# One transformer block on one core: attention in a hand-written order, router logits with the weights held in the array, and a first gather with the tokens held in the array

## The chip, the cores and the metric

The kernel runs on one core of one Trainium2 chip. The metric is device time in microseconds (us) of one execution; lower is better. The core has five engines that run in parallel, each through its own list of instructions in order, and wait for each other by semaphores: TensorE (PE in the rows; its weight loads, PEld, stand apart), VectorE (DVE), ScalarE (ACT), GpSimd (POOL) and SyncE (SP), which issues nearly all DMA transfers here. PE writes only to PSUM, which ACT and DVE read.

## The reference

The block works on 512 latent tokens of width 1024 with 256 context tokens. Cut to what matters:

```python
# sub-layer 1
h = modulate(rms_norm(x, g_pre1), sh1, sc1);  hc = ... the same for ctx
na_o = neighbourhood_attention(q, k, v, k_ctx, v_ctx, rpb)   # 8 heads of 64
hg_o = hgrn2_readout(...)                                    # 4 heads of 128, a scan over the tokens
mix  = jnp.concatenate([na_o, hg_o], axis=-1) @ w_out
x    = x + gt1 * rms_norm(mix, g_post1)
# sub-layer 2
h2   = modulate(rms_norm(x, g_pre2), sh2, sc2)
aff  = jax.nn.softmax(h2 @ w_router, axis=-1)                # 512 tokens x 16 experts
gate, idx = lax.top_k(aff.T, 64)                             # each expert picks its 64 best tokens
xs   = h2[idx]
y    = (silu(xs @ w_gate[e]) * (xs @ w_up[e])) @ w_down[e] * gate    # 16 experts, 1024 -> 2752 -> 1024
x    = x + gt2 * rms_norm(scatter_add(y, idx), g_post2)
```

## The kernel before

**Stages.** The first part computes the projections and the scan (until about 340 us). Then come attention and the output projection with all that follows it for the four blocks of 128 tokens (numbered j = 0 to 3), then the 16 experts one after another, whose weights (some 540 MB) stream from HBM.

**Memory.** Large tiles come from a heap of 18 slots of 1 MB (`big`). A weight tile of an expert can only be loaded when the tile that lay in its slot before has been read for the last time. Five smaller places (`wk`, `wx`) hold weight tiles too. SP issues the loads in the order in which the program names them, so a load that waits for its slot holds up those behind it. In the order of use the first expert's tiles are four for each of five steps over 512 hidden columns, two small ones for the last 192 columns, then eleven of `w_down`. In both programs 20 tiles of the first expert go in before PE has used one.

**Attention.** There are 16 units (j, hp): a block of 128 queries and a pair of heads. A unit passes through score products (`att_a`: PE, then DVE's fused add and minimum at L843 and ACT's exponential at L845), division by the sum (`att_n`, DVE L850 and L851), four transposes for each head and their copy (`att_b`, PE L856, ACT L858), and the product with the values (`att_c`, PE L867). Step n of `attention` runs these for units n, n-1, n-2 and n-3; there are 19 steps, 0 to 18. PSUM holds two score tiles and two transposed tiles at a time (`aux`, four buffers).

**Other work in those steps.** `out_state` multiplies the scan's result with its half of `w_out` (eight pieces of 12 matmuls); `finish(j)` does the attention's half (24 matmuls), the norm, the residual and the router's logits and softmax of block j; `before_last` prepares block 3; `project` does block 3's output projection head pair by head pair; `ranks_first` counts, for the first expert, how many tokens rank above each token. They are generators in the list `side`, and `tick` advances the first of them by two or three pieces a step. Up to the end of the attention the framework's scheduler may then reorder what each engine is given; from `drain()` on the program's order holds.

**Behind the attention.** `finish_last` norms block 3 and computes its logits and softmax; then `select(0)` ranks the remaining tokens, makes a one-hot matrix `hot` (tokens x 64 places) of the first expert, and `gather_one` gathers: before, 32 matmuls with a 128x128 piece of the tokens `res[j]` as the weights and 64 columns of `hot` streamed past them, the result already turned with the features on the partitions; `normed` scales it into `xT`. `expert(0)` then starts (L1291), and the second expert's gather runs in the middle of it.

In the trace a matmul of 32-bit floats leaves two records (the 32 matmuls of `gather_one` are x64); those of the split type F32R leave one.

## Time and profile before

| | us |
|---|---|
| median of 3 runs | 1773.34 (1771.5 to 1775.71) |
| the profiled execution, its own time | 1774.09 |
| its span, first to last instruction | 1772.3 |
| around the span | 1.8 |

The profiled execution is 0.75 us above the median. Times below are us from the start of its span. A row of the trace gives the start, the length, the engine and line, the operation, output <- input, shapes and a count of records that follow each other; in brackets the idle time just before and what ended it. Granted clock is that of PE as a share of 2.4 GHz.

### The profile page before, as it was taken

The page shows a single profiled execution, that of the slowest core. Times are in us where ns is not written, and L with a number is a line of the kernel's source. Part 1 is how long each engine was busy: PE and PEld are TensorE (multiplying, and loading weights), DVE is VectorE, ACT ScalarE, POOL GpSimd, SP SyncE. Part 2 cuts the span into 40 slices and gives each one's busy share as a digit, 9 for nine tenths or more (in the row PEclk, how much of TensorE's full clock was granted, in tenths as well). Part 3 has the DMA queues.
Part 4 walks back from the last instruction along what each step waited for, and adds up shares of the span by engine and source line. Part 5 has one row for each costly group of instructions (what it writes and reads, how often), then busy time and mean ns, then how long its engine had stood idle before and what let it go on. Part 6 is the DMA issues. An engine that isn't in the chain of part 4 may idle for free.

```text
span 1772.3 us, 21446 instructions
## 1 busy us (share of the span) xinstructions
PE 1598.9 (90%) x8726; PEld 840.6 (47%) x8726; DVE 599.6 (34%) x1259; ACT 343.2 (19%) x669; POOL 185.8 (10%) x291
## 2 busy tenths in 40 slices
PE   7999989999799999989898889889898988898896
PEld 5988789777643433433242334334332423343233
DVE  4787653765521311402221130204122211302023
ACT  4463331564310110101011001101100110111002
POOL 1262463622000000000000000000000000000003
PEclk9999999998799999999999999999999999999998
DMA  9463212541678999999999999999999999999995
GB/s 379 158 228 117 95 49 85 157 167 60 272 313 345 420 421 421 421 421 420 421 420 422 420 421 420 421 421 420 421 421 421 420 420 421 422 420 421 420 421 232
DMA packets 91059, 602.45 MB, mean 340 GB/s; under 512 B 12992, under 2 KB 13376, under 8 KB 23888
## 3 DMA queue, kind: packets, MB, share of 16 engines
q1 hardware_dynamic: 90176, 598.73, 82.5%
q0 software_dynamic: 784, 2.34, 0.4%
q8 instruction: 69, 1.13, 0.3%
q14 instruction: 30, 0.25, 0.0%
HBM read 598.10 MB, written 3.16 MB: 339 GB/s over the span
## 4 chain that ended last, share of the span: by engine, by line
DMA 52%; PE 29%; DVE 3%; issue 2%; POOL 2%; ACT 1%; POOLq 0%; SPq 0%; DVEq 0%; ACTq 0%
DMA w_up<-in_w_gu_dram 21%; DMA w_gate<-in_w_gu_dram 14%; DMA w_down<-in_w_dn_dram 13%; PE mm L1291 10%; PE o L1320 4%; DMA wx<-in_w_gu_dram 2%; PE aux L1188 2%; PE mm L463 2%; PE mm L802 2%; PE aux L1199 1%; PE mm L454 1%; DMA w_down<-in_w_dl_dram 1%; PE o L1356 1%; PE aux L856 1%; PE o L867 1%
## 5 line engine op out<-in xcount | busy, mean ns | idle before, releaser
L1291 PE MATMUL mm<-w_up,room 128*64 128x512 f32 (+1 forms) x1264 | 511.7, 553 | 61.4 <-DMA w_up<-in_w_gu_dram 61.4
L1291 PE MATMUL mm<-w_gate,room 128*64 128x512 f32 (+1 forms) x1152 | 453.2, 542 | 0.0
L1320 PE MATMUL o<-w_down,hidT 128*64 128x512 f32 (+1 forms) x1320 | 306.4, 600 | 25.6 <-DMA w_down<-in_w_dn_dram 24.7
L1291 PEld LDWEIGHTS mm<-w_up,room 128*64 128x64 f32 x1264 | 164.9, 138 | 227.1 <-issue 113.7
L1291 PEld LDWEIGHTS mm<-w_gate,room 128*64 128x64 f32 x1152 | 151.0, 137 | 155.4 <-issue 137.2
L1300 DVE TENSOR_TENSOR sl<-sl,mm 64x512 f32<-64x512 f32 x96 | 60.9, 634 | 441.7 <-ACT sl L1296 441.1
L1267 DVE COPY hidT<-aux 128x256 f32<-128x256 f32 x96 | 38.6, 402 | 503.4 <-PE aux L1266 503.4
L1296 ACT ACTIVATE sl<-mm 64x512 f32<-64x512 f32 x96 | 52.4, 546 | 727.4 <-PE aux L1266 574.0
L1320 PEld LDWEIGHTS o<-w_down,hidT 128*64 128x64 f32 (+1 forms) x1320 | 85.3, 136 | 222.4 <-issue 145.1
L1291 PE MATMUL mm<-wx,room 128*64 128x512 f32 x384 | 172.9, 597 | 0.0
L1291 PE MATMUL mm<-wk,room 128*64 128x512 f32 (+1 forms) x272 | 119.9, 592 | 5.8 <-DMA wk<-in_w_gu_dram 5.8
L1241 POOL COPY hot<-room 128x256 f32<-128x256 f32 x2 | 0.8, 450 | 1064.0 <-DMA wx<-in_w_gu_dram 1064.0
L454 PE MATMUL mm<-hl,whi 128*128 128x512 f32 x320 | 102.6, 399 | 0.6 <-ACT fk L709 0.6
L1328 ACT ACTIVATE y<-o 64x512 f32<-64x512 f32 x30 | 17.7, 591 | 329.8 <-PE o L1320 329.4
L1372 PE MATMUL mm<-yy,back 128*128 128x512 f32 (+1 forms) x128 | 48.0, 459 | 23.4 <-DVE sl L1300 21.7
L1291 PEld LDWEIGHTS mm<-wx,room 128*64 128x64 f32 x384 | 49.5, 136 | 39.3 <-issue 34.5
L454 PEld LDWEIGHTS mm<-hl,whi 128*128 128x128 f32 x320 | 58.8, 189 | 12.5 <-ACT fk L709 1.1
L454 PE MATMUL mm<-hl,wlo 128*128 128x512 f32 x160 | 63.0, 394 | 0.0
L1266 PEld LDWEIGHTS aux<-cc,sl 64*128 64x128 f32 x352 | 28.9, 137 | 69.4 <-issue 51.5
L1188 PE MATMUL aux<-room,res 128*128 128x128 f32 x448 | 53.7, 278 | 1.5 <-DVE room L1165 1.5
L1188 PEld LDWEIGHTS aux<-room,res 128*128 128x128 f32 x448 | 51.1, 192 | 2.5 <-issue 1.6
L1291 PEld LDWEIGHTS mm<-wk,room 128*64 128x64 f32 x272 | 33.1, 141 | 30.1 <-issue 16.6
(342 smaller groups left out, 2036.5 us busy)
## 6 DMA issues: line engine op xcount, KB each, us to landing
w_down<-in_w_dn_dram SPq DMA_DIRECT2D x150, 1024.0 KB
w_up<-in_w_gu_dram SPq DMA_DIRECT2D x128, 1024.0 KB
w_gate<-in_w_gu_dram SPq DMA_DIRECT2D x114, 1024.0 KB
wx<-in_w_gu_dram SPq DMA_DIRECT2D x48, 1024.0 KB
wk<-in_w_gu_dram SPq DMA_DIRECT2D x30, 1024.0 KB
wm<-in_w_mod_dram SPq DMA_DIRECT2D x24, 1024.0 KB
wraw<-in_w_in_dram SPq DMA_DIRECT2D x16, 1024.0 KB
w_down<-in_w_dn_dram SPq DMA_DIRECT2D x15, 768.0 KB
```

The lines of the kernel that those rows point to most:

```text
L454: T.matmul(p, w[wx][:, k, a], hT(hx, k, t0, t1), start=(n == 0), stop=(n == 3 * KT - 1))
L463: T.matmul(p, hT(hx, k, t0, t0 + 128), w[wx][:, k, :], start=(n == 0), stop=(n == 3 * KT - 1))
L802: T.matmul(p, lhs[lx][:, 2 * k2 + k], w[k2][wx][:, k, n * 512:(n + 1) * 512], start=(m == 0), stop=(m == 11))
L856: T.transpose(pT[:, i], s[:, i * 128:(i + 1) * 128], ident)
L1188: T.matmul(pX[:, k], res[j][:, (4 * k4 + k) * 128:(4 * k4 + k + 1) * 128], hot[:, 4 + j], start=(j == 0), stop=(j == 3))
L1266: T.transpose(pT[:, f], sl[:, f * 128:f * 128 + 128], ident[0:64, 0:64])
L1267: V.tensor_copy(hid[:, f0:f0 + nf], pT[:, 0:nf])
L1291: T.matmul(p[64 * g:64 * g + 64, 0:n], xe[k], ws[g][k // 4][:, k % 4, 0:n], start=(k == 0), stop=(k == KT - 1))
L1296: S.activation(sl[:, 0:n], p[0:64, 0:n], AF.Silu)
L1300: V.tensor_mul(sl[:, 0:n], sl[:, 0:n], p[64:128, 0:n])
L1320: T.matmul(pd[64 * g:64 * g + 64], hid[r, f0 + f], ww[r], start=(f0 + f == 0), stop=(f0 + f == 21))
L1372: T.matmul(p, back[:, j * 128:(j + 1) * 128], yn[i], start=(i == 0), stop=(i == 1))
```

## The change

Four things are edited.

The order of attention is written out. `att_a` falls into `att_bias`, `att_s`, `att_m` and `att_e`; in step n PE gets the scores of unit n, the value product of unit n-3 and the transposes of unit n-2, in this order; DVE divides unit n-1 and then does the minimum of unit n. The scheduler is switched off before step 2, so the program's order holds on every engine. The side work comes from a table `plan`: for each step the pieces that follow it, in order. The split of the attention's half of `w_out` into a high and a low part (`wout_split`) becomes pieces of that table, and block 3's head pairs are projected one in each of the steps 16 to 18 and one after them. The high and low parts of the heads (`nhl`) move into the heap.

The router's logits are computed with the router weights as the stationary operand: eight matmuls of 128x32 weights against 128 streamed tokens into four groups of 32 columns (`products`), a copy to SBUF, and one matmul with `sel4` that adds the four groups up and turns the result. This replaces eight matmuls with 128x128 tokens as weights and 16 streamed columns. It applies to the shift's logits, the four blocks and block 3's residual, six times in all.

The first two gathers are by token: for each j the 64 columns of `hot` are the weights and 512 columns of `res[j]` are streamed, twice (8 matmuls); ACT copies the result, PE turns it with four transposes, and `normed` scales it. For the first expert the matmuls of j = 0 to 2 are given before the last ranks.

`finish_last` gets 12 matmuls whose result nobody reads (`warm`), the ranks of the first three blocks are done in three pieces (after step 18, after the last projection, and inside `finish_last`), and one pass over the second half of block 3 moves from DVE to ACT.

```diff
+    def wout_load(k2):
         raw = big((128, 2, D), "woraw")
         nc.sync.dma_start(raw, I["w_out"][k2])
+        return raw
+
+    def wout_split(raw, to):
         hi = big((128, 2, D), "wohi", F32R)
         lo = big((128, 2, D), "wolo", F32R)
+        to.append((hi, lo))
...
+            yield
...
+    wr = np_.tile([128, KT, 32], F32, name="wr")
+    G.memset(wr, 0.0)
+    nc.sync.dma_start(wr[:, :, 0:NE], I["w_router"].rearrange("(k p) e -> p k e", p=128))
+    sel4 = np_.tile([128, NE], F32, name="sel4")
+    V.tensor_reduce(sel4, ident.rearrange("p (g c) -> p c g", g=4)[:, 0:NE], axis=mybir.AxisListType.X, op=OP.add)
...
+            if n >= 3:
+                att_c(*units[n - 3], B.pop(n - 3))
             if 0 <= n - 1 < len(units):
                 for a in A[n - 1]:
                     att_n(*a)
+            if n < len(units):
+                A[n] = att_m(p)
...
+                for a in A[n]:
+                    att_e(*a)
+            yield n
...
+    ctx.enter_context(tc.manual_schedule())
...
+    def products(x):
+
+        pl = aux((128, 128))
+        for k in range(KT):
+            g = 32 * (k % 4)
+            T.matmul(pl[g:g + 32], wr[:, k], x(k), start=(k < 4), stop=(k >= 4), tile_position=(0, g))
+        lg = np_.tile([128, 128], F32, name="lg", bufs=1)
+        V.tensor_copy(lg, pl)
+        yield
+        pr_ = aux((128, NE))
+        T.matmul(pr_, lg, sel4, start=True, stop=True)
+        yield pr_
...
+    def parts_of_heads():
+        nhl = big((128, 2, 4, 128), "nhl", F32R)
+        return nhl[:, 0], nhl[:, 1]
...
-        pr_ = aux((128, NE))
-        for k in range(KT):
-            T.matmul(pr_, hT2[:, k], wr[:, k], start=(k == 0), stop=(k == KT - 1))
-        yield pr_
+        yield
+        yield from products(lambda k: hT2[:, k])
...
+    def warm(n):
+
+        p = otl((128, 256))
+        for i in range(n):
+            T.matmul(p, ident, cc[:, 0:256], start=True, stop=True)
...
+        warm(2)
         for n, c in enumerate(halves):
             S.activation(junk, p[n], AF.Square, accum_out=q(n))
             V.tensor_mul(x1[:, c], p[n], g1[:, c])
-        products = router(x1)
-        next(products)
-        next(products)
-        c = halves[0]
-        V.scalar_tensor_tensor(junkv, x1[:, c], 2.0, xr3[:, c], op0=OP.mult, op1=OP.mult, accum_out=q(3))
-        S.activation(junk, x1[:, c], AF.Square, accum_out=q(5))
-        rnorm_of(q(0), q(1), q(2))
-        c = halves[1]
-        V.scalar_tensor_tensor(junkv, x1[:, c], 2.0, xr3[:, c], op0=OP.mult, op1=OP.mult, accum_out=q(4))
-        V.scalar_tensor_tensor(junkv, x1[:, c], 1.0, x1[:, c], op0=OP.mult, op1=OP.mult, accum_out=q(6))
-        pr_ = next(products)
+        logits = router(x1)
+        next(logits)
...
+        between()
+        next(logits)
+        pr_ = next(logits)
...
+        warm(8)
...
-        if j == 3 and hp > 1:
-            for i in range(0 if hp == 2 else hp, hp + 1):
-                project(j, i)
-        if hp == 3 and j < 3:
-            side.append(finish(j))
-            if j == 1:
-                side.append(before_last())
-            if j == 2:
-                side.extend([ranks_first(0), ranks_first(1)])
...
-    side.append(shift_logits())
-    for n, _ in enumerate(att):
-        tick(2 if n < 6 else 3)
-    ctx.enter_context(tc.manual_schedule())
-    drain()
-    finish_last()
...
+    def ranks_first():
+
+        first["row"] = row = otl()
+        first["rk"] = rk = keep.tile([128, 4, 6], F32, name="rk4")
+        G.memset(rk, 0.0)
+        spread(0, row, 0, 2)
+        ranks(0, row, rk, range(2), 0, 256, 0)
+        yield
+        spread(0, row, 2, 3)
+        ranks(0, row, rk, range(2), 256, 384, 2)
+        yield
+        ranks(0, row, rk, [2], 0, 384, 0)
+        yield
+
+    def na_weights():
+        raws = [wout_load(k2) for k2 in range(2)]
+        yield
+        for raw in raws:
+            for n, _ in enumerate(wout_split(raw, wo_na)):
+                if n % 4 == 3:
+                    yield
+
+    na_w, shift, last3, rank1 = na_weights(), shift_logits(), before_last(), ranks_first()
+    fin = [finish(j) for j in range(3)]
+    st = state_part
+    plan = {
+        2: [st, st, na_w], 3: [st, st], 4: [st, shift], 5: [st, shift], 6: [st], 7: [st, na_w],
+        8: [na_w, na_w, fin[0]], 9: [na_w, fin[0]], 10: [fin[0], fin[0]], 11: [fin[0], fin[1], last3],
+        12: [fin[0], fin[1]], 13: [fin[0], fin[1], fin[1], last3], 14: [fin[0], fin[1], last3, fin[2]],
+        15: [fin[2], fin[2], fin[1], last3], 16: [fin[2], fin[1], 0], 17: [fin[2], fin[1], 1],
+        18: [fin[2], fin[2], rank1, 2],
+    }
+    for n in att:
+        for a in plan[n]:
+            if isinstance(a, int):
+                project(3, a)
+            else:
+                next(a, None)
+    project(3, 3)
+    next(fin[2], None)
+    next(rank1)
+    finish_last(lambda: next(rank1))
...
-        def gather_one(i):
-            for k2 in range(4):
-                pX = aux((128, 2, CAP))
-                for k in range(2):
-                    for j in range(4):
-                        T.matmul(pX[:, k], res[j][:, (2 * k2 + k) * 128:(2 * k2 + k + 1) * 128], hot[:, 4 + j, i],
-                                 start=(j == 0), stop=(j == 3))
-                for k in range(2):
-                    normed(2 * k2 + k, xT[:, 2 * k2 + k, i], pX[:, k], k == 0)
+        def gather_one(i, pG, js):
+            for j in js:
+                for g in range(2):
+                    T.matmul(pG[64 * g:64 * g + 64], hot[:, 4 + j, i], res[j][:, g * 512:(g + 1) * 512],
+                             start=(j == 0), stop=(j == 3))
+            if js[-1] < 3:
+                return
+            xg = mp.tile([128, 512], F32, name="xg", tag="back", bufs=2)
+            S.activation(xg, pG, AF.Copy)
+            pX = aux((128, 4, 2, CAP))
+            for k in range(4):
+                T.transpose(pX[:, k].rearrange("p g c -> p (g c)"), xg[:, k * 128:(k + 1) * 128], ident)
+            for k in range(KT):
+                normed(k, xT[:, k, i], pX[:, k % 4, k // 4], k % 2 == 0)
...
+                pG = aux()
+                gather_one(i, pG, [0, 1, 2])
+                ranks(e, row, rk, [3], 384, 512, 4)
...
+                if i:
+                    gather_one(i, aux(), [0, 1, 2, 3])
+                else:
+                    gather_one(i, pG, [3])
```

What this does to the engines' order is seen at three places.

ACT, steps 7 to 9 of the attention. Before, the eight pieces of the second `w_out` half (`wohi`) stand in one run behind the copy `nhi` of block 0's heads (L1010), ahead of the next transposed tiles (`sT`, L858):

```order
L845 ACTIVATE s,mn<-s,mn 128x512 x2
L858 ACTIVATE sT<-aux 128x512 x2
L1010 ACTIVATE nhi<-o 128x512
L792 ACTIVATE wohi<-woraw 128x256 x8
L858 ACTIVATE sT<-aux 128x512 x2
L845 ACTIVATE s,mn<-s,mn 128x512 x2
L1023 ACTIVATE x_3249,sj<-res_3239 128x512 x2
```

Of the change, the same place:

```order
L796 ACTIVATE wohi<-woraw 128x256 x4
L880 ACTIVATE sT<-aux 128x512 x2
L869 ACTIVATE s,mn<-s,mn 128x512 x2
L796 ACTIVATE wohi<-woraw 128x256 x8
L1052 ACTIVATE nhl<-o 128x512
L880 ACTIVATE sT<-aux 128x512 x2
L869 ACTIVATE s,mn<-s,mn 128x512 x2
L796 ACTIVATE wohi<-woraw 128x256 x4
L1063 ACTIVATE x_3254,sj<-res_3244 128x512
```

The last four pieces now stand behind the exponentials of unit 9 (L869), and block 0's first squares (L1063), which need the product with them, right behind.

DVE, from the high and low parts of block 3's last heads to the first pass over block 3. Before (`nlo` are the low parts, L1107 and L1110 the ranks, L1067 the first pass, over `mm`, block 3's projection):

```order
L1002 TENSOR_SCALAR affs<-affs,sm 128x16
L1107 TENSOR_SCALAR cmp,rk_4327<-o,affs 128x384
L1110 SCALAR_TENSOR_TENSOR cmp,rk_4327<-o,affs,bef 128x384
L973 TENSOR_TENSOR nlo<-o,nhi 128x128
L1107 TENSOR_SCALAR cmp,rk_4327<-o,affs 128x384
L1110 SCALAR_TENSOR_TENSOR cmp,rk_4327<-o,affs,bef 128x384
L1067 TENSOR_TENSOR res_3240<-mm,gx 128x512
```

Of the change:

```order
L1157 SCALAR_TENSOR_TENSOR cmp,rk_4338<-o,affs,bef 128x256
L1019 TENSOR_TENSOR nhl<-o,nhl 128x128 x2
L190 TENSOR_SCALAR rsx<-sj 128x1
L1077 SCALAR_TENSOR_TENSOR affs<-aux,rsx,cr 128x16
L1040 TENSOR_REDUCE sm<-affs 128x1
L1044 RECIPROCAL sm<-sm 128x1
L1045 TENSOR_SCALAR affs<-affs,sm 128x16
L1154 TENSOR_SCALAR cmp,rk_4338<-o,affs 128x128
L1157 SCALAR_TENSOR_TENSOR cmp,rk_4338<-o,affs,bef 128x128
L1154 TENSOR_SCALAR cmp,rk_4338<-o,affs 128x128
L1157 SCALAR_TENSOR_TENSOR cmp,rk_4338<-o,affs,bef 128x128
L1113 TENSOR_TENSOR res_3245<-mm,gx 128x512 x2
```

Block 2's softmax (L1077 to L1045) and four rank instructions now stand between the last low parts and the first pass; before, the softmax stood ahead of the last low part.

PE, from block 3's last projection to the first expert. Before (L987 transposes block 3, L992 its logits, L1116 spreads its affinities, L1199 the gather):

```order
L979 MATMUL mm<-wohi,nlo 128x512
L987 MATMUL aux<-cc,res_3240 128x128 x8
L992 MATMUL aux<-wr,hT_4360 128x16 x8
L1116 MATMUL o<-cc,affs 128x128
L1199 MATMUL aux<-room,res_3239 128x64 x2
L1199 MATMUL aux<-room,res_3240 128x64 x2
```

Of the change:

```order
L994 MATMUL aux<-sel_2994,lg 128x16
L1163 MATMUL o<-cc,affs 128x128
L1101 MATMUL o<-cc 128x256 x2
L1033 MATMUL aux<-cc,res_3245 128x128 x8
L1101 MATMUL o<-cc 128x256 x2
L989 MATMUL aux<-hT_4386,wr 32x128 x8
L994 MATMUL aux<-sel_2994,lg 128x16
L1101 MATMUL o<-cc 128x256 x8
L1163 MATMUL o<-cc,affs 128x128
L1258 MATMUL aux<-res_3244,room 64x512 x4
L1258 MATMUL aux<-res_3245,room 64x512 x4
L1266 MATMUL aux<-cc,xg 128x128 x4
```

The gather is 8 matmuls and 4 transposes in place of 32 matmuls, and the unread ones (L1101) stand around the logits.

## Rows read from the trace of the kernel before

**Rows 1.** The page, the span in 40 equal slices: what the DMA engines moved.

```profile
GB/s 379 158 228 117 95 49 85 157 167 60 272 313 345 420 421 421 421 421 420 421 420 422 420 421 420 421 421 420 421 421 421 420 420 421 422 420 421 420 421 232
```

**Rows 2.** Busy time of each engine in stretches: stretch and its length, busy us (count) of PE, PEld, DVE, ACT and POOL, granted clock, DMA share, GB/s.

```profile
470.00:475.00 5.00, 0.47 (x1) 0.18 (x1) 3.85 (x17) 1.74 (x6) 0.77 (x1) 0.50 0.91 362
480.00:485.00 5.00, 5.00 (x25) 5.00 (x25) 0.61 (x2) 0.81 (x2) 0.00 (x0) 0.50 1.02 431
490.00:495.00 5.00, 5.00 (x16) 2.14 (x17) 0.34 (x1) 1.69 (x2) 0.00 (x0) 0.50 0.00 0
...
535.00:540.00 5.00, 5.00 (x38) 2.75 (x36) 1.28 (x3) 0.97 (x2) 0.00 (x0) 1.00 0.78 267
```

**Rows 3.** SP's issues of weight loads: start, length.

```profile
473.29 0.38 SPq L1286 DMA_DIRECT2D w_up<-in_w_gu_dram  x1
497.14 3.76 SPq L1277 DMA_DIRECT2D wk<-in_w_gu_dram  x2
...
534.26 0.33 SPq L1286 DMA_DIRECT2D w_up<-in_w_gu_dram  x1
```

**Rows 4.** The chain of work that ended last, from the first gather to the first matmul with `w_down`: start, length, what.

```profile
476.89 1.54 PE aux L1199 x6
478.44 12.64 PE aux L1199 x58
491.08 9.47 PE mm L1291 x32
...
501.13 7.02 PE mm L1291 x32
...
523.35 7.29 PE aux L1199 x64
...
542.66 5.30 PE o L1320 x24
```

**Rows 5.** The same chain in attention, the start of step 3 (first row), step 4 (the next five) and the start of step 8 (last).

```profile
348.31 0.63 PE aux L836 x4
...
357.08 0.63 PE aux L836 x4
357.71 0.43 PE aux L838 x4
358.15 1.02 PE aux L856 x8
359.17 1.02 PE o L867 x16
360.19 5.66 PE mm L802 x24
...
388.45 0.63 PE aux L836 x4
```

**Rows 6.** Groups of instructions by line and shape from 329 to 480 us: busy us, mean ns of one | idle time before.

```profile
L845 ACT ACTIVATE s<-s,mn 128x512 f32<-128x512 f32 x32 | 22.8, 715 | 17.5 <-DVE mn L843 17.5
L843 DVE CUSTOM_DVE_ANT_0 s<-aux,bias 128x512 f32<-128x512 f32 x32 | 21.0, 687 | 18.6 <-PE aux L838 18.4
L851 DVE TENSOR_SCALAR s<-s,mn 128x512 f32<-128x512 f32 x32 | 19.6, 623 | 0.8
L858 ACT ACTIVATE sT<-aux 128x512 f32<-128x512 f32 x32 | 17.7, 582 | 4.0 <-PE aux L856 4.0
L793 DVE TENSOR_TENSOR wolo<-woraw,wohi 128x256 fp32r<-128x256 f32 x32 | 15.8, 561 | 1.9 <-ACT wohi L792 1.9
L1110 DVE SCALAR_TENSOR_TENSOR cmp<-o,affs,bef 128x384 bf16<-128x384 f32 x4 | 2.5, 616 | 0.1
L1110 DVE SCALAR_TENSOR_TENSOR cmp<-o,affs,bef 128x128 bf16<-128x128 f32 x4 | 1.4, 344 | 0.0
```

**Rows 7.** Timeline of PE: 16 records (8 matmuls) of router logits; 24 records (12 matmuls) with weights of 32 columns in four column groups and 256 streamed columns, early in the kernel.

```profile
435.48 1.96 PE L992 MATMUL aux<-wr,hT 128*128 128x16 f32 x16
38.63 1.50 PE L274 MATMUL o<-wm,sc 128*32 128x256 f32 x24
```

**Rows 8.** PE's granted clock in two stretches of attention (columns as in rows 2), and eight transposes at either clock (timeline).

```profile
400.00:410.00 10.00, 9.91 (x47) 7.34 (x46) 5.18 (x17) 4.77 (x12) 2.59 (x4) 0.66 0.00 0
...
420.00:430.00 10.00, 8.96 (x49) 6.97 (x49) 4.90 (x18) 6.11 (x18) 3.37 (x6) 0.72 0.15 52
...
380.62 1.09 PE L856 MATMUL aux<-cc,s 128*128 128x128 f32 x8
397.32 1.02 PE L867 MATMUL o<-sT,vo 128*64 128x128 f32 x7 [0.92 <-ACT sT L858]
403.50 1.97 PE L856 MATMUL aux<-cc,s 128*128 128x128 f32 x8
```

**Rows 9.** Timeline from the end of block 3's projection to the first one-hot matrix: the first instruction of block 2's softmax, the last projection, the first pass, block 3's affinities, the one-hot of blocks 0 to 2.

```profile
456.51 0.23 DVE L1038 SCALAR_TENSOR_TENSOR affs<-aux,rsx,cr 128x16 f32<-128x16 f32 x1 [1.85 <-PE aux L992]
463.58 0.39 PE L979 MATMUL mm<-wohi,nlo 128*128 128x512 f32 x1
464.09 0.69 DVE L1067 TENSOR_TENSOR res<-mm,gx 128x512 f32<-128x512 f32 x1 [0.31 <-ACT x L1066]
472.01 0.23 DVE L1002 TENSOR_SCALAR affs<-affs,sm 128x16 f32<-128x16 f32 x1
476.48 0.36 DVE L1165 TENSOR_TENSOR room<-room,rsx 128x192 f32<-128x192 f32 x1
```

More of the change, by code (lines that the diff above doesn't have):

```diff
@@ L793, in wout @@
             V.tensor_sub(lo[:, k, c], raw[:, k, c], hi[:, k, c].bitcast(F32))
-        return hi, lo
+            yield
+    def wout(k2):
+        to = []
+        for _ in wout_split(wout_load(k2), to):
+            pass
+        return to[0]
     def outproj(p, lhs, w, n):
@@ L827, in att_a @@
         win = cc[:, C_WIN + 32 * var:C_WIN + 32 * var + 32]
-        pa = [slice(64 * g, 64 * g + 64) for g in range(2)]
         for g in range(2):
@@ L832, in att_a, with att_s @@
                          rpb[:, 2 * hp + g, off:off + 256].rearrange("p (r b c) -> p r b c", r=8, b=4))
+    def att_s(j, hp):
+        c0 = (0, 8, 24, 32)[j]
+        pa = [slice(64 * g, 64 * g + 64) for g in range(2)]
         p = [aux(), aux()]
@@ L868, in att_c @@
                          start=(i == 0), stop=(i == 3))
+    units = [(j, hp) for j in range(4) for hp in range(4)]
     def attention():
-        units = [(j, hp) for j in range(4) for hp in range(4)]
         A, B = {}, {}
@@ L965, in moe_block @@
     early = {}
+    def parts_of_heads():
+        nhl = big((128, 2, 4, 128), "nhl", F32R)
+        return nhl[:, 0], nhl[:, 1]
     def project(j, hp):
         if hp == 0:
-            early[j] = ([np_.tile([128, 4, 128], F32R, name=nm, bufs=1) for nm in ("nhi", "nlo")], [mmt(), mmt()])
+            early[j] = (parts_of_heads(), [mmt(), mmt()])
         (nhi, nlo), p = early[j]
@@ L1012, in finish @@
         nc.gpsimd.dma_start(xr1, I["xb"][j * 128:(j + 1) * 128, :])
-        if not wo_na:
-            wo_na.extend([wout(0), wout(1)])
         yield
@@ L1118, in moe_block @@
     first = {}
[L1120 to L1147 removed]
+    def ranks_first():
[4 more added lines that the diff above has]
+        ranks(0, row, rk, range(2), 0, 256, 0)
+        yield
+        spread(0, row, 2, 3)
[9 more added lines that the diff above has]
+                if n % 4 == 3:
+                    yield
+    na_w, shift, last3, rank1 = na_weights(), shift_logits(), before_last(), ranks_first()
[18 more added lines that the diff above has]
+    finish_last(lambda: next(rank1))
     if "aff" in dbg:
@@ L1209, in select @@
                 ranks(e, row, rk, [3], 0, 384, 0)
-                ranks(e, row, rk, range(3), 384, 512, 2)
+                ranks(e, row, rk, range(3), 384, 512, 4)
                 one_hot(hot, rk, i, 0, 3)
-                ranks(e, row, rk, [3], 384, 512, 2)
+                pG = aux()
+                gather_one(i, pG, [0, 1, 2])
+                ranks(e, row, rk, [3], 384, 512, 4)
                 last_factor()
```

56 lines of the change are left out of this document (22 added, 34 removed).

## The prediction, made before the changed kernel ran

> **What bounds the kernel now.** First the DMA row of the page: from the fourteenth slice on, some 575 us, the transfers run at 420 to 422 GB/s and hardly vary [rows 1]. That part moves expert weights and the change does not touch it, so the end is fixed by the moment from which the stream has no more gaps. Next the stretches around that moment: the stream stands still at 490 to 495 us and moves 267 GB/s at 535 to 540 [rows 2]. Who makes the gaps is seen in SP's issues: after the 20 tiles of the first expert (the last issued at 473.29) the next goes out at 497.14, when the first matmuls have read their tiles, and one at 534.26, after the second gather [rows 3]. So PE frees the slots late. The chain that ended last says the same: from the first gather at 476.89 to the first `w_down` matmul at 542.66 it is PE's [rows 4]. Whatever brings PE earlier to that matmul brings the end earlier by as much, as long as the 20 tiles are there in time. I therefore sum what the change does to PE up to there, in three parts, against the profiled execution; its 1774.09 us lie 0.75 above the median and 1.8 above its span, and I apply the sum to the median.
>
> **Part 1, attention up to the end of block 3's projection (t0).** Before, t0 is 463.58 + 0.39 = 463.97 [rows 9].
> One unit costs PE 0.63 + 0.43 + 1.02 + 1.02 = 3.10 us, a piece of 12 matmuls of the output projection half of 5.66, 2.83 [rows 5]. DVE has 2 x (0.69 + 0.62) a unit [rows 6], with small ones some 3.15; ACT 2 x (0.72 + 0.58) = 2.6.
> New logits: a row of weights 32 columns wide has 1.50 us for 12 matmuls over 256 streamed columns, so eight over 256 cost 1.0 and, if time goes with columns, 0.5 over 128; the old eight cost 1.96 [rows 7]. I take 0.5 plus 0.25 for the sum with `sel4`; the saving is 1.2 each (0.7 at the upper bound). The copy between them is a DVE instruction with other PE work behind it.
> Steps 3 to 7 are PE's: 3.10 + 5.66 = 8.8 for step 3 (before 357.08 - 348.31 = 8.8 [rows 5]), then 6.4 and 6.2 (one piece and the shift's logits), 5.9 and 5.9. From 348.3, step 8 starts at 381.5. The old step 8 starts at 388.45 [rows 5], but two projection pieces (5.7) are done by then that the new one still has; the rest, 1.2, is the saved logits.
> From step 8 I add each step's PE work and the waits that its order makes:
> Steps 8 and 9, 14.4. PE has only 3.1 + 6.1, but the second projection piece needs the last four split pieces, and these stand on ACT behind unit 9's exponentials. DVE: 3.15, eight pieces at 0.56 [rows 6] (some of it hidden in ACT's) and a 0.69 low part come to 7.9; the next unit brings 11.0; exponentials, four pieces and DVE's half of them end at 13.2, five matmuls at 14.4.
> Step 10, 6.1 (PE). Step 11, 5.9: the next scores need the buffers that DVE's minimum frees, and DVE has an addition and two multiplications (2.3 to 2.5) ahead of its 3.15. Step 12, 7.1 (3.10 + transposes 1.03 + 2.97) and step 13, 7.6 (PE). Step 14, 5.0 (DVE, as step 11). Step 15, 11.5: two projection pieces wait 1.2 for block 2's low part on DVE, then 5.9, transposes and a sum. Steps 16 and 17, 5.8 and 5.0: each projection of a head pair waits for its low part behind finishing work on DVE. Step 18 and the last head pair, 8.4: transposes, their copies, logits, then DVE's four ranks over 256 columns (about 1.9, between the 0.34 and 0.62 of [rows 6]) ahead of the last two low parts, then ten matmuls.
> Sum 76.8, t0 = 458.3, 5.7 earlier.
> The clock: before, PE was granted 0.66 of full speed at 400 to 410 and 0.72 at 420 to 430; eight transposes took 1.97 us instead of 1.09 there, after a wait of 0.92 for ACT [rows 8]. These 6.2 us are in the old time, and in mine none is. The new order has longer waits but no logits of 16 columns; I charge 0.7, a quarter of one such dip: **part 1 is -5.0**. Bounds: -10 (steps 8, 9 and 15 at their PE work) and 0 (the old stalls and dips come back, or half a microsecond more in each of eleven steps).
>
> **Part 2, from t0 to the end of the first cut.** Before: 463.97 to 472.24 for block 3's affinities, to 476.84 for the first one-hot matrix [rows 9], 491.08 for the first expert matmul and 500.55 for the end of its first cut [rows 4]: 8.3, 12.9, 27.1 and 36.6 after t0.
> The change puts block 2's sum and softmax (before from 456.51 on [rows 9], ahead of t0), the spread and four ranks of 128 columns ahead of the first pass on DVE: 2.0 + 0.4 + 4 x 0.29, so the pass starts 3.6 after t0 instead of 0.1. Inside the chain, two ranks of 384 columns (1.25) and a copy come in, and the shorter logits and a pass that moved to ACT go out; I count +0.2. The one-hot matrix is there at 12.9 + 3.5 + 0.2 = 16.6 after t0.
> The gather: 64 records took 14.19 us, at 0.50 of the clock all through, and the same 64 take 7.29 at full clock [rows 2, 4]. Sixteen records of 512 columns cost 7.02 / 32 x 16 = 3.5 at full clock, twice that at half; then ACT's copy 0.6, four transposes 0.5, the first `normed` 0.4, half a microsecond of handing over: 5.5, or 9 at half throughout. PE stands idle for some 4 us ahead of it, as before, when the clock was at 0.50 from 470 on [rows 2]; the unread matmuls end well before. But the old first cut took 9.47 us against 7.02 of the next [rows 4], so the clock came back within it; the new gather is work of that cut's kind and should begin to bring it back itself. I take 6.4.
> The Trainium skill, TensorE: Matmul & The Clock Gate, section Why this matters for your kernels, says the same of the idle time (it drops the clock) and would begin the gather at half rate in spite of the unread matmuls; by it this term is up to 7.5, by the unread matmuls alone 5.5. The row at 470 us speaks for the page.
> So the first expert matmul starts 23.0 after t0 (-4.1), and its cut takes 7.1 instead of 9.47 (-2.4): **part 2 is -6.5**. Bounds: -7.5 (full clock) and -1.2 (half clock through gather and cut).
>
> **Part 3, to the first `w_down` matmul.** The second gather falls from 7.29 to 3.5 + copy, transposes and scaling with their waits, 5.0, which PE takes in order: **-2.3**. Its six other cuts are unchanged.
>
> **Are the tiles there?** Slots come free in another order, 12 tiles instead of 11 at the end of attention. By the order of SP's loads the first of them waits for the projection in step 17, about 450, and the rest for t0 and what follows it, the last for ACT's final squares at t0 + 13. At 1 MB in 2.5 us (421 GB/s) 12 take 30, so they are in at 481, while the first cut ends near 489 and the tiles of the last full cut are wanted 20 us later. Eight microseconds of slack: hidden.
> Around all this, `memset`, `sel4` and the second reads cost nothing: POOL and DVE are idle there. The unread matmuls cost PE time in which it waits.
>
> **Sum.** -5.0 - 6.5 - 2.3 = -13.8: 1773.34 - 13.8 = 1759.5 us. On the profiled execution: span 1758.5.
>
> **Rivals.**
> More waits than I count: the program's order leaves no engine a way around a late operand, and every step has one or two hand-overs that I take as 0.1 to 0.2. At t0 no earlier than before, 464 to 468, parts 2 and 3 remain: 1764 to 1769. For it: the old order was made to dodge such waits and still had 0.5 to 1 us stalls [rows 8].
> Fewer: if steps 8, 9 and 15 hide their waits and the clock stays up, t0 is 453 to 455 and the gain 19 to 25, until the weight stream itself binds: 1749 to 1754. For it: DVE and ACT are half idle on the average.
> Slower, by the clock in steps 8 to 18: PE has some 63 us of full-clock work there, and at half clock each costs another. To turn -13.8 into +3.6 it takes 17 us of it at half, three times the 6.2 lost before [rows 8]. For it: the waits in steps 8, 9, 11 and 14 leave PE half idle for 4 us at a time. Time: 1778 or more. The skill's page on the clock gate speaks for this case, since it makes idle stretches the cause; in the rows dips of 10 us followed on stalls of about 1.
> No change, because the gap at 535 to 540 is not PE's but that of the slots' order, and the stream starts no earlier: 1773. Against it: the load at 534.26 goes out just when the cut after the gather has read its tile [rows 3, 4].
>
> **How the numbers follow.** The sum as worked out, 1754 to 1764: 0.50, which gives the predicted time. More waits, 1764 to 1769.8: 0.22. Fewer, below 1754: 0.18. Within 0.2% (3.5 us, about what a measurement of this kernel can tell from no change): 0.06. Slower: 0.04. Faster is then 0.90. The range 1750 to 1769 leaves out the two last, some 0.04 of each neighbour, and nothing of the first.
>
> **What would show it.** Right: block 3's last projection ends at 455 to 462; step 9's projection waits for split pieces; the one-hot matrix follows 16 to 17 us after t0; the first expert matmul 22 to 25 after it; the first cut near 7 us; the second gather 5. Wrong: a granted clock near 0.5 for more than 10 us in steps 8 to 18, a stream that stands still in front of the first cut for want of slots, or a time that changes in the experts' part.

## The result, and the profile after

| | before | changed |
|---|---|---|
| median | 1774.15 us | 1763.4 us |
| range of the runs | 1771.5 to 1776.02 | 1762.4 to 1767.99 |
| ratio, 95% interval | | 0.9946 (0.9931 to 0.9961) |
| span of the profiled execution | 1772.3 us | 1761.5 us |

The change makes the kernel 10.7 us faster by the medians, 10.8 by the spans and 9.6 by the ratio, which compares the means. Forecast were 13.8 us and 1759.5.

The bound is still the weight stream. Here are stretches of the changed kernel (columns as in [rows 2]):

```profile
475.00:480.00 5.00, 1.56 (x6) 0.59 (x8) 4.43 (x25) 0.00 (x0) 0.55 (x1) 0.93 1.00 416
480.00:485.00 5.00, 4.24 (x16) 1.29 (x12) 0.00 (x0) 0.60 (x1) 0.00 (x0) 0.73 0.98 413
490.00:495.00 5.00, 5.00 (x26) 1.76 (x24) 1.46 (x4) 0.59 (x1) 0.00 (x0) 1.00 0.67 203
535.00:540.00 5.00, 5.00 (x26) 1.69 (x24) 0.29 (x1) 0.00 (x0) 0.00 (x0) 1.00 0.53 187
```

At 480 us the granted clock, 0.50 before, is 0.73, and at 490 the stream is running again. The issues of SP that answer to [rows 3] (start, length):

```profile
474.52 0.33 SPq L1357 DMA_DIRECT2D w_up<-in_w_gu_dram  x1
489.37 3.76 SPq L1348 DMA_DIRECT2D wk<-in_w_gu_dram  x2
...
524.14 0.33 SPq L1357 DMA_DIRECT2D w_up<-in_w_gu_dram  x1
```

After the first expert's last tile the next load goes out at 489.37 in place of 497.14. The chain that ended last, as in [rows 4]:

```profile
478.44 5.37 PE aux L1258 x16
483.89 0.61 ACT xg L1263
484.54 0.67 PE aux L1266 x4
485.24 0.41 ACT room L1240
485.69 7.09 PE mm L1362 x32
...
515.58 3.61 PE aux L1258 x16
519.21 0.61 ACT xg L1263
519.86 0.66 PE aux L1266 x4
520.52 7.02 PE mm L1362 x32
...
532.54 5.30 PE o L1391 x24
```

The first gather (L1258) starts 1.55 us later than before, but its matmuls, the copy, the transposes and the scaling take 7.25 us in place of 14.2, the first cut (L1362) 7.09 in place of 9.47 and the second gather 4.94 in place of 7.29. The first `w_down` matmul is at 532.54, 10.1 us earlier, and the end with it.

Attention, in which the prediction put 5.0 us, gives less. The last projection of block 3 ends at 461.7 (before 463.97 [rows 9]):

```profile
450.12 0.50 PE L1025 MATMUL mm<-wohi,nhl 128*128 128x512 f32 x1 [2.42 <-ACT nhl L1018]
...
457.86 0.73 PE L1025 MATMUL mm<-wohi,nhl 128*128 128x512 f32 x2 [2.00 <-DVE nhl L1019]
...
461.09 0.63 PE L1025 MATMUL mm<-wohi,nhl 128*128 128x512 f32 x1
```

These are PE's waits in steps 17 and 18 and the last matmul of the projection. DVE's first pass over block 3 (L1113) starts 3.2 us after t0, and the first one-hot matrix (L1226) is ready 16.7 after it:

```profile
464.91 1.28 DVE L1113 TENSOR_TENSOR res<-mm,gx 128x512 f32<-128x512 f32 x2
...
478.02 0.36 DVE L1226 TENSOR_TENSOR room<-room,rsx 128x192 f32<-128x192 f32 x1
```

### The profile page after: what moved, and what is told of

It reads as the page before. It is cut to its first block, busy times and chain, and to the rows that moved or that the text cites. A ratio compares the mean times of both kernels' runs of the same rounds, so it can differ in the third digit from the quotient of the medians.

```text
span 1761.5 us, 21371 instructions
## 1 busy us (share of the span) xinstructions
PE 1574.5 (89%) x8674; PEld 813.5 (46%) x8674; DVE 597.6 (34%) x1272; ACT 345.4 (20%) x673; POOL 185.4 (11%) x293
## 4 chain that ended last, share of the span: by engine, by line
DMA 47%; PE 33%; DVE 4%; issue 2%; POOL 2%; ACT 2%; POOLq 0%; SPq 0%; DVEq 0%; ACTq 0%
DMA w_gate<-in_w_gu_dram 18%; DMA w_up<-in_w_gu_dram 17%; PE mm L1362 13%; DMA w_down<-in_w_dn_dram 11%; PE o L1391 4%; PE aux L1249 3%; PE mm L812 2%; PE mm L463 2%; DMA wx<-in_w_gu_dram 1%; PE mm L454 1%; PE o L1427 1%; PE aux L1337 1%; DVE wolo L797 1%; PE o L889 1%; DMA woraw<-in_w_out_dram 1%
## 5 line engine op out<-in xcount | busy, mean ns | idle before, releaser
L1362 PE MATMUL mm<-w_up,room 128*64 128x512 f32 (+1 forms) x1264 | 506.9, 548 | 64.1 <-DMA w_up<-in_w_gu_dram 64.1
L1362 PE MATMUL mm<-w_gate,room 128*64 128x512 f32 (+1 forms) x1152 | 453.8, 542 | 0.0
L1362 PEld LDWEIGHTS mm<-w_up,room 128*64 128x64 f32 x1264 | 163.6, 137 | 224.6 <-DMA w_up<-in_w_gu_dram 115.1
L1362 PEld LDWEIGHTS mm<-w_gate,room 128*64 128x64 f32 x1152 | 151.1, 137 | 159.0 <-issue 141.2
L1362 PE MATMUL mm<-wx,room 128*64 128x512 f32 x384 | 172.9, 597 | 0.0
L1362 PE MATMUL mm<-wk,room 128*64 128x512 f32 (+1 forms) x272 | 114.4, 568 | 6.3 <-DMA wk<-in_w_gu_dram 5.8
L1362 PEld LDWEIGHTS mm<-wx,room 128*64 128x64 f32 x384 | 49.5, 136 | 39.8 <-issue 35.0
L454 PEld LDWEIGHTS mm<-hl,whi 128*128 128x128 f32 x320 | 58.8, 189 | 12.9 <-ACT fk L709 1.6
L463 PE MATMUL mm<-whi,hl 128*128 128x256 f32 x256 | 47.2, 286 | 0.0
```

The lines of the kernel that those rows point to most:

```text
L454: T.matmul(p, w[wx][:, k, a], hT(hx, k, t0, t1), start=(n == 0), stop=(n == 3 * KT - 1))
L463: T.matmul(p, hT(hx, k, t0, t0 + 128), w[wx][:, k, :], start=(n == 0), stop=(n == 3 * KT - 1))
L1362: T.matmul(p[64 * g:64 * g + 64, 0:n], xe[k], ws[g][k // 4][:, k % 4, 0:n], start=(k == 0), stop=(k == KT - 1))
```

## The experiments

The start of step 3 of attention lies between 348.2 and 351.7 us in the profiles of all kernels, though the code ahead of it is the same or nearly so; the last section has part of the reason. The stretches below therefore count from there, read from PE's timeline: from the first score matmul of step 3 to t0, to the first gather matmul, to the first expert matmul, to the first `w_down` matmul, and their sum. The end came 1229 to 1231 us after that last point in all 14 profiles, so the sum stands for the part of the time that the edits reach. Where a median is given, the kernel before measured 1774.2 to 1775.4 beside it.

| kernel | to t0 | to gather | to expert | to `w_down` | sum | ratio to before (95%) |
|---|---|---|---|---|---|---|
| before | 115.7 | 12.9 | 14.1 | 51.6 | 194.4 | 1 |
| changed | 112.7 | 16.7 | 7.3 | 46.8 | 183.5 | 0.9946 (0.9931 to 0.9961) |
| e1_old_logits | 120.6 | 13.6 | 7.1 | 46.8 | 188.1 | 0.9976 (0.9967 to 0.9985) |
| e2_old_gather | 115.7 | 16.6 | 14.1 | 50.9 | 197.3 | 1.0015 (1.0005 to 1.0025) |
| e3_no_warm | 112.5 | 16.5 | 8.0 | 46.8 | 183.8 | 0.9949 (0.9935 to 0.9964) |
| e4_order_only | 120.5 | 13.9 | 14.1 | 50.2 | 198.8 | 1.0039 (1.0027 to 1.0052) |
| e5_before_gather | 115.7 | 12.9 | 8.3 | 46.8 | 183.7 | 0.9942 (0.9930 to 0.9955) |
| e6_before_logits | 109.5 | 14.8 | 14.0 | 50.3 | 188.6 | 0.9985 (0.9976 to 0.9994) |
| e7_split_early | 114.1 | 15.3 | 7.3 | 46.8 | 183.5 | 0.9942 (0.9930 to 0.9955) |
| e8_ranks_moved | 109.7 | 15.5 | 8.0 | 46.8 | 180.1 | 0.9939 (0.9926 to 0.9953) |
| e9_more_warm | 112.6 | 16.8 | 5.6 | 46.8 | 181.7 | 0.9935 (0.9923 to 0.9948) |
| e10_together | 111.2 | 17.2 | 5.6 | 46.8 | 180.7 | 0.9927 (0.9906 to 0.9947) |
| e11_before_logits_gather | 109.5 | 14.8 | 8.2 | 46.8 | 179.2 | 0.9919 (0.9907 to 0.9932) |
| e12_before_all_warm | 109.5 | 14.5 | 5.6 | 46.8 | 176.3 | 0.9901 (0.9885 to 0.9917) |

The question was which of the four edits the gain belongs to: my sum gave 5.0 to attention and the logits, 8.8 to what stands behind them.

**One edit taken back.**

e1_old_logits:

```diff
-        pl = aux((128, 128))
...
+        pr_ = aux((128, NE))
+        for k in range(KT):
+            T.matmul(pr_, x(k), wr[:, k, 0:NE], start=(k == 0), stop=(k == KT - 1))
+        yield
         yield pr_
```

> The changed kernel with the router's logits taken back to eight matmuls of 16 streamed columns with the tokens as weights, and no copy and second matmul; nothing else. Theory A (the sum of parts): each of the six costs PE 1.2 us more, of which those in steps where PE waits anyway are hidden, so 4 to 7 us more than the change: 1767 to 1770, and the granted clock stays near 1.00 in attention. Rival B (the narrow matmuls are what takes the clock away): stretches of 5 us and more at 0.50 come back around the logits of blocks 0 and 1, as at 400 and 424 us before, and the time is 1772 or more.

Measured 0.9976: 5.3 us more than the change (0.0030 of 1774), which is Theory A's. One stretch of low clock came back (0.56 to 0.59 from 398 to 402), not two. e4_order_only (0.50 from 400 to 402) and, with the new logits, e2_old_gather (0.50 too) lost it at the same place, so in the written order the narrow matmuls are not needed for that.

e2_old_gather: the loop of 32 matmuls from the kernel before in `gather_one`, called once for each expert.

> The changed kernel with both first gathers taken back to 32 matmuls with the tokens as weights and 64 streamed columns; the unread matmuls stay. Theory A: the gather runs at half the clock again, 14.2 us in place of 7.25, the first cut 9.5 in place of 7.1, the second gather 7.3 in place of 4.9; about 11 more, 1773 to 1775, all of the measured gain of the change. Rival B (the unread matmuls keep the clock): the first gather takes 7.3 to 9, the time is 1766 to 1768.

Measured 1.0015: the gain is gone and a little more. The gather takes 14.1 us, at a granted clock of 0.50 from 484 to 498, in spite of the unread matmuls. Rival B falls. Theory A's 11 us are in the profile, 6.9 in the gather and 4.1 behind it; 3.0 more are in the stretch to t0, whose instructions are those of the changed kernel.

e3_no_warm: the calls of `warm` taken out.

> The changed kernel without the 12 matmuls that nobody reads. Theory A: the clock is at half for the 4 us in front of the gather with or without them; the gather may lose the 1.8 us that it now has over half clock and the first cut up to 2.4: 0 to +4, 1763 to 1767. Rival B (they keep PE at full clock for block 3's transposes, logits and the gather): more than +4, and block 3's transposes and logits get longer too.

Measured 0.9949, no difference that can be told from the change. The gather takes 8.0 us in place of 7.3, the cut 7.09 as with them: Theory A, at its low end, though not for its reason. Without the unread matmuls the granted clock is 0.50 from 462 to 485 us, through most of the gather; with them it is 1.00 from 470 up to the gather and falls within it, as shown under part 2 below. Block 3's logits (L989) take 1.41 us in place of 0.64, its transposes 1.94 in both, and the stretch to the gather is no longer for it (16.5).

e4_order_only: the edits of e1, e2 and e3 at once.

> The changed kernel with old logits, old gathers and no unread matmuls: what stays of the change is the written order, the moved ranks and the pass on ACT. Theory A: from the two traces the order ends block 3's projection 2.3 us earlier, but that holds the logits' 4 to 6; and the moved softmax and ranks put the one-hot matrix 3.8 us later after it. So it is slower than the kernel before: 1777 to 1783. Rival B (the order is worth something by itself, since no clock dips remain in it): 1768 to 1774.

Measured 1.0039, 7 us slower than before. So the order, the moved ranks and the pass on ACT together lose time: Theory A.

**One edit alone on the kernel before.**

e5_before_gather: the new `gather_one` and its calls, put into the kernel before.

> The kernel before with the new gathers alone. Theory A: the first gather at half clock takes 9 in place of 14.2 us, the first cut 7 to 9.5, the second gather 4.9 in place of 7.3: 7.5 to 10 us off, 1764 to 1767, so nearly all that the whole change gives. Rival B (the gain needs the order and the unread matmuls): 2.4 to 5 us off, 1769 to 1772.

Measured 0.9942, 10.3 us off and as much as the whole change: Theory A, just past its range. The chain, first and second gather with the cut behind each, and the first `w_down` matmul:

```profile
477.85 6.41 PE aux L1197 x16
484.35 0.60 ACT xg L1202
485.00 0.67 PE aux L1205 x4
486.15 7.09 PE mm L1301 x32
...
516.04 3.61 PE aux L1197 x16
...
533.00 5.30 PE o L1330 x24
```

Even from half the clock (6.41 us for 16 records that take 3.61 later), the gather ends 5.8 us sooner than the old one, and the cut behind it runs at full clock.

e6_before_logits: `products`, `wr` with 32 columns and `sel4`, put into the kernel before; `nhi` and `nlo` move into the heap, since the pool has no room for the new tiles otherwise.

> The kernel before with the new logits alone (the heads' high and low parts lie in the heap as in the change, since the room is not there otherwise). Theory A: 1.2 us for each of the logits that PE does not hide, 4 to 6 off, 1768 to 1770. Rival B (the narrow matmuls take the clock away): the stretches at 0.50 around 400 and 424 us vanish too, 8 to 11 off, 1763 to 1766. Rival C (the copy between the two products is a wait that takes back what they save): within 2 of the time before.

Measured 0.9985, 2.7 us off, less than Theory A's 4 to 6. In the profile t0 is 6.2 sooner and no clock is lost where it was lost before, which is Rival B's sign without its price (columns as in [rows 8]):

```profile
400.00:410.00 10.00, 9.31 (x73) 6.66 (x74) 5.88 (x18) 4.70 (x12) 3.08 (x5) 1.00 0.61 238
420.00:430.00 10.00, 8.28 (x70) 5.57 (x71) 6.45 (x21) 7.43 (x20) 3.05 (x5) 1.00 0.11 44
```

The same stretches in e5_before_gather, which has the old logits:

```profile
400.00:410.00 10.00, 10.00 (x50) 7.58 (x50) 4.19 (x14) 3.77 (x10) 1.59 (x3) 0.66 0.00 0
420.00:430.00 10.00, 8.18 (x47) 6.22 (x46) 5.01 (x16) 6.39 (x19) 3.11 (x5) 0.77 0.16 54
```

In the scheduler's order the lost clock goes with the old logits: the two profiles that have them (before and e5) needed 115.7 us to t0, the three with the new ones (e6, e11 and e12) lost no clock up to t0 and needed 109.5. PE's rows of logits in that stretch take 5.9 us in place of 11.4. How much of the 6.2 is this, how much the clock, and how much the other order that the scheduler makes of the new rows, can't be told.

But the stretch to the gather grows by 1.8: there the second product of block 3's logits stands on the path and waits for the copy between the two:

```profile
465.82 0.40 PE L967 MATMUL aux<-sel,lg 128*128 128x16 f32 x2 [2.48 <-DVE lg L965]
```

The median gains less than the sum's 5.8: step 3 begins 1.9 us later in this profile than in that of the kernel before, which the sum leaves out, and the profiled execution lies 1.5 us below the median of its eleven.

e11_before_logits_gather: both of them.

> The kernel before with the new logits and the new gathers together, so the change without its written order, without the moved ranks and without unread matmuls. Measured from step 3 to the first matmul with w_down, the gathers alone gave 10.7 us and the logits alone 5.8, the whole change 10.9. Theory A (they add up, and the written order takes the logits' part back): 16 off, 1757 to 1759, faster than the change. Rival B (the two share a gain, that of the clock in front of the first expert, or the tiles are not there sooner): 1762 to 1764, as the change.

Measured 0.9919, some 1760, 4.8 us better than the change: Theory A, just past its range (15.1 of its 16 us by the sum). What the change has besides, the written order with the moved ranks, the unread matmuls and the pass on ACT, costs these 4.8. Two other pairs say the same: the changed kernel with old logits lies 6.0 above e5 (0.9976 and 0.9942), and e4, which has the order, the ranks and the pass alone, 6.9 above the kernel before. By the sums of the table the three pairs give 4.2, 4.4 and 4.4. No run has the written order without the other two; e8_ranks_moved, below, bears on that. PE's waits, from step 3 to t0, show where. First the changed kernel (what waited, for what: us in total, times, longest):

```profile
PE mm L812 <- ACT wohi L796: 2.8, 1, 2.8
PE mm L1025 <- ACT nhl L1018: 2.4, 1, 2.4
PE mm L1025 <- DVE nhl L1019: 2.0, 1, 2.0
PE mm L812 <- ACT nhl L1052: 1.8, 2, 1.3
```

Then the kernel with the old order and the new logits:

```profile
PE o L870 <- ACT sT L861: 1.7, 3, 0.9
PE aux L839 <- ACT sT L861: 0.8, 1, 0.8
PE mm L802 <- ACT nhl L1023: 0.7, 1, 0.7
```

And PE's busy time in the same stretch (columns as in [rows 2]), changed kernel first:

```profile
349.01:461.72 112.71, 99.27 (x777) 74.83 (x776) 60.67 (x180) 61.94 (x157) 23.91 (x37) 0.99 0.31 118
```

```profile
349.30:458.77 109.47, 104.27 (x778) 75.38 (x777) 63.21 (x179) 61.77 (x158) 23.66 (x34) 1.00 0.30 109
```

The written order makes PE idle for 13.4 us (112.71 - 99.27) where the scheduler's has 5.2. It gets 5.0 of that back in busy time, with the same matmuls in longer runs of one kind: the products with the values take 20.3 us in 16 runs in the written order, 26.3 in 24 runs in the scheduler's. That the longer runs are the reason is not shown.

**The waits of the written order.**

e7_split_early:

```diff
-        2: [st, st, na_w], 3: [st, st], 4: [st, shift], 5: [st, shift], 6: [st], 7: [st, na_w],
-        8: [na_w, na_w, fin[0]], 9: [na_w, fin[0]],
+        2: [st, st, na_w], 3: [st, st], 4: [st, shift], 5: [st, shift, na_w], 6: [st, na_w], 7: [st, na_w],
+        8: [na_w, fin[0]], 9: [fin[0]],
```

> The changed kernel with the four pieces of wout_split one or two steps earlier in the plan (steps 5, 6, 7 and 8 in place of 7, 8, 8 and 9). Theory A: PE waits 1.3 and 2.8 us in step 9 for the heads' high part and for the split pieces behind the exponentials on ACT; without that block 3's projection ends 4 us earlier, and so does all that follows: 1758.5 to 1760. Rival B: the pieces take DVE and ACT in steps 5 to 8 as much as they did in 8 and 9, or steps 11 and 14 wait the longer: 1762 to 1764.

Measured 0.9942, the sum unchanged: Rival B by the time, for a reason that neither named. PE's wait moves to step 7 (2.36 us, for the minimum on DVE), where DVE stands in front of the first low part of the second weight:

```profile
376.84 1.43 DVE L797 TENSOR_TENSOR wolo<-woraw,wohi 128x256 fp32r<-128x256 f32 x4 [6.64 <-PE aux L854]
```

That `wolo` lies in the heap slot of `qb0`, the queries of blocks 0 and 1, whose last reader is the score product of step 7 (L854); no plan of these pieces alone can have it sooner. (In this profile the clock was lost at 380 and 452 us too, so what the earlier pieces would have gained without that stays open.)

e8_ranks_moved:

```diff
-        18: [fin[2], fin[2], rank1, 2],
+        18: [fin[2], fin[2], rank1],
...
-    project(3, 3)
-    next(fin[2], None)
-    next(rank1)
-    finish_last(lambda: next(rank1))
+    project(3, 2, 0)
+    project(3, 3, 0)
+    next(fin[2], None)
+    project(3, 2, 1)
+    project(3, 3, 1)
+    next(rank1)
+    finish_last(lambda: (next(rank1), next(rank1)))
```

Here `rank1` yields once more after its first spread, and `project` with 0 does the high and low part, with 1 the matmuls.

> The changed kernel with another order around the last two head pairs: both low parts of block 3 first, block 2's sum and softmax next, then the projections of the two head pairs, the four ranks over 256 columns beside them, and the four over 128 columns after the first passes. Theory A: the projection no longer waits 2.0 us for the low part behind ranks, and the first pass no longer 3.3 us for block 2's softmax and ranks: 4 to 5 us off, 1758 to 1760. Rival B: the ranks only change their place on DVE, whose chain to the one-hot matrix is the bound: the time from step 3 to the one-hot matrix falls by less than 2, 1761.5 to 1764.

In the profile t0 is 3.0 sooner and the stretch to the gather 1.2 shorter, 4.2 in all, as Theory A has it; the gather lost 0.7 of it to the clock. The ratio is 0.9939 beside 0.9946, a gain of 1.2 us within the intervals, which is Rival B's time: the profile has the gain in one execution, the times do not show it. With 109.7 us to t0 the written order is here level with the scheduler's (109.5 in e6 and e11). So in this profile what the change loses ahead of t0 hangs on the place of the ranks and the clock behind their wait, not on the order of the attention; by the ratios (0.9939 and 0.9919) 3.5 us still lie between this kernel and e11.

e9_more_warm:

```diff
                 spread(e, row, 3, 4)
+                warm(9)
```

> The changed kernel with nine more unread matmuls behind the last spread of affinities, so that PE is busy up to the first gather. Theory A (the clock falls because PE waits 4.1 us for the one-hot matrix): the gather's matmuls take 3.6 in place of 5.4 us, 1761 to 1762.5. Rival B: unread matmuls don't hold the clock, or they end late and the gather starts later: 1763 to 1765.

```profile
481.06 3.68 PE aux L1258 x16
```

The gather's matmuls take 3.68 us in place of 5.37, and the steps up to the first expert 5.6 in place of 7.3: Theory A. The ratio, 0.9935, is 2 us lower, within the intervals.

e10_together: e8 and e9 at once.

> The changed kernel with the new place of the ranks and the nine further unread matmuls at once. From step 3 to the first w_down matmul the one measured 3.4 less than the change, the other 1.8. Theory A (they add up): 178.3 us from step 3, and 1759 to 1761 measured beside 1774 to 1775 before. Rival B: the ranks' new place leaves PE idle elsewhere, the clock falls there, and the unread matmuls run at half and delay the gather: 180 to 182 from step 3, 1762 to 1764.

Measured 0.9927, 1761.27, at the edge of Theory A's range, but the sum is Rival B's 180.7. PE at the sum of block 3's logits, and the unread matmuls behind it:

```profile
467.93 0.61 PE L994 MATMUL aux<-sel,lg 128*128 128x16 f32 x2 [2.22 <-DVE lg L991]
468.38 5.10 PE L1104 MATMUL o<-cc 128*128 128x256 f32 x16
473.31 0.27 PE L1166 MATMUL o<-cc,affs 128*128 128x128 f32 x1
```

The ranks now keep DVE from the logits' copy and PE waits 2.22 us. Behind that its clock is at 0.50, the eight unread matmuls take 5.10 us instead of the 3.70 of the changed kernel, and the spread of the affinities (L1166) stands behind them. That is Rival B's path, but the wait alone does not make it: e8_ranks_moved has the same instructions up to there and the same wait, and the clock stayed at 1.00:

```profile
468.04 0.40 PE L994 MATMUL aux<-sel,lg 128*128 128x16 f32 x2 [2.22 <-DVE lg L991]
468.28 3.70 PE L1104 MATMUL o<-cc 128*128 128x256 f32 x16
```

The stretch to t0 is 1.5 us longer than in e8, with the clock at 0.57 from 396 to 400, where e8 had 1.00. So whether the two edits add up is not settled by this profile.

e12_before_all_warm: e11 with unread matmuls in the four waits behind block 3's projection.

```diff
         V.tensor_copy(lg, pl)
+        if fill[0]:
+            warm(fill[0])
...
+        warm(2)
         logits = router(x1)
+        fill[0] = 4
...
+                warm(5)
                 spread(e, row, 3, 4)
+                warm(8)
```

> The kernel before with new logits, new gathers and unread matmuls in the four waits of PE between block 3's projection and the first gather (2, 4, 5 and 8 of them), in the old order of the attention and of the ranks. Logits and gathers alone measured 179.2 us from step 3, with the gather at half the clock from its start (8.2 us for its three steps). Theory A: at full clock these take 5.5, the other things stay: 176.5 from step 3, 1756.5 to 1758.5. Rival B: the first unread matmuls run at half the clock themselves and hold up the spread and the gather: 178 to 181, 1759 to 1762.

Measured 0.9901, 1758.06 (1756.09 to 1758.59): better than the kernel before and the changed one, and the sum, 176.3, is that of Theory A. In the profile no stretch of attention or of the work behind it lost the clock. The gather of e11, then that of this kernel:

```profile
473.53 6.33 PE L1210 MATMUL aux<-res,room 128*64 128x512 f32 x16 [4.21 <-DVE room L1178]
```

```profile
473.33 3.65 PE L1222 MATMUL aux<-res,room 128*64 128x512 f32 x16 [0.66 <-DVE room L1190]
```

It takes 3.65 us behind work and 6.33 behind a wait of 4.21.

## Why the prediction was right, and where it was not

**What bounds the kernel** held: the end kept its distance of 1230 us from the first `w_down` matmul in every profile, and the tiles were there in time. The last of the first expert's 20 was issued at 474.52 and the stream ran until 485, four microseconds later than I had it, with no cut waiting.

**Part 1** is the term that was mis-sized: -5.0 forecast, -2.3 by the absolute t0, -3.0 from step 3. Its steps held up to the end of step 16: step 8 starts 32.8 us after step 3 (forecast 33.2), step 10 47.7 (47.6, with the waits of 1.3 and 2.8 us in step 9 that the sum has), step 15 79.0 (79.3), step 17 96.4 (96.6). The miss is in the last two. "Steps 16 and 17, 5.8 and 5.0": step 17 took 6.3, since PE waits 2.42 not for the low part on DVE but for the high part on ACT (L1018), which stands behind squares and the softmax's exponential. "Step 18 and the last head pair, 8.4": 10.0; the four ranks made a wait of 2.00 as forecast, but the ten matmuls behind it took 3.9 us, against some 2.5 at full clock in e8 (12 in 3.0). Of the clock I charged 0.7 for all steps; in this profile it cost nothing in steps 3 to 16 and about 1.4 here. That is in part luck: of the four profiles with these instructions three (the change, e3 and e9) took 112.5 to 112.7 us to t0, the fourth (e2) 115.7, as long as the kernel before.

What the sum hid is that part 1 holds two things of opposite sign. I priced the logits' saving and the order's waits in one row of steps and never asked what the order does without the logits. The rival with more waits named the reason, "the program's order leaves no engine a way around a late operand", but I gave it to a t0 no earlier than before. The runs show it, together with the moved ranks and the pass on ACT, as a loss of 4 to 7 us in each pair, covered by the logits; how much of it is the order's own stays open (e8).

**Part 2** (-6.5, measured -5.5: 31.1 from t0 to the end of the first cut in place of 36.6) was right in two of its steps: one-hot matrix 16.7 after t0 (16.6), cut 7.09 (7.1). The third, the gather, took 7.25 against 6.4, and not on the path that I gave it, from half the clock upwards. PE had waited 4.1 us for the one-hot matrix; the gather then began at full clock, fell to half about a microsecond later, with PE busy, and was back at full by 483 us (columns as in [rows 2]):

```profile
478.50:479.00 0.50, 0.50 (x4) 0.22 (x6) 0.50 (x6) 0.00 (x0) 0.00 (x0) 1.00 1.01 426
480.00:481.00 1.00, 1.00 (x4) 0.24 (x2) 0.00 (x0) 0.00 (x0) 0.00 (x0) 0.50 1.09 459
483.00:484.00 1.00, 0.79 (x4) 0.00 (x0) 0.00 (x0) 0.11 (x1) 0.00 (x0) 1.00 1.01 426
```

In e9 and e12, in which PE has work up to the gather, its steps took 5.6 us, the 5.5 of the other case. The page of the Trainium skill (TensorE: Matmul & The Clock Gate, Why this matters for your kernels), which has idle time take the clock, gave up to 7.5 for the change and was nearer than my value, though the gather did not begin at half rate.

One bound of part 2 was worked out wrongly: half the clock through gather and cut would be 9 and 14.0 us, some 3 us more than before and not 1.2 less. No profile came near it.

**Part 3** was exact: 4.94 for the second gather, -2.35.

**The rivals.** "Slower, by the clock in steps 8 to 18" did not come in the profile of the change, but its mechanism exists: e2_old_gather has the same instructions up to the gather and needed 3.0 us more to t0, with the clock lost three times. That the change does nothing falls with e5. The case of fewer waits was added up wrongly: a t0 of 453 to 455 with the other parts as forecast gains 18 to 20 us, not 19 to 25. The measured time lies within the likeliest case, 1754 to 1764, at its upper end. The six signs set down for it all came, the first at its edge (461.7 of 455 to 462).

## What to carry to other kernels

Ask of every edit in a bundle what it does alone, and with its companions already there: here a written order that, with its moved ranks, lost 4 to 7 us hid behind two edits that gained. Taking those edits back one at a time showed each gain; the loss showed only where the order stood alone (e4) or its companions stood without it (e11). When a short product stands alone between two waits, turn it so that few matmuls stream many columns, and fill the wait ahead of it on PE with work whose result nobody reads, if that work ends before the operand comes. Before moving a piece earlier in an order, look up who last read the buffer it writes to.

## What the runs showed of the hardware that was not expected

The same instructions keep or lose PE's clock from one execution to the next. From 395 to 405 us the changed kernel and e2_old_gather, which is 2.0 us behind there, run the same order (columns as in [rows 2]); first the changed kernel:

```profile
395.00:405.00 10.00, 9.66 (x76) 7.19 (x77) 6.50 (x18) 4.84 (x13) 0.00 (x0) 1.00 0.12 29
```

```profile
395.00:405.00 10.00, 7.65 (x45) 5.73 (x46) 5.28 (x17) 5.31 (x15) 1.41 (x2) 0.83 0.01 2
```

The granted clock is 1.00 in the one and 0.83 in the other, part of it at 0.50. The same goes for the part ahead of attention; the changed kernel and e3_no_warm, whose code is the same there:

```profile
245.00:250.00 5.00, 4.41 (x33) 4.20 (x33) 2.35 (x8) 0.38 (x1) 5.00 (x14) 1.00 0.01 3
```

```profile
245.00:250.00 5.00, 3.38 (x12) 3.38 (x13) 1.72 (x6) 0.00 (x0) 5.00 (x15) 0.66 0.01 3
```

Step 3 starts at 349.0 and 351.5 in these two, so 2.5 of the 3.3 us between their spans arose before the edited code began. The clock is not all of it: e6_before_logits lost none from 40 to 345 us and began step 3 at 350.1. A profile's absolute times should not be compared without a common start. Nor did every wait in PE's work cost the clock: after one of 2.83 us that ended at 395 it stayed at 1.00, after one of 2.00 that ended at 457.86 it was at 0.50 from 460 to 462, and after the same wait of 2.22 us it stayed at 1.00 in e8 and was at 0.50 in e10.
